# A decoder trunk's feed-forward stage: ordinary work in ready pieces, held transposes, second products added onto used banks

## The chip, the cores and the metric

The kernel runs on one core of a Trainium2 chip. The core has a matrix engine (TensorE, PE in the profile; its weight loads are PEld), a vector engine (VectorE, DVE), a scalar engine (ScalarE, ACT), a general one (GpSimd, POOL) and a queue engine (SyncE, SP) that issues most transfers here. Each engine works through its own list of instructions and waits on semaphores for the others. The metric is the device time of one execution in microseconds (us); lower is better.

## The reference

Two decoder layers over 256 tokens of width 2048, all in float32:

```python
for l in range(DEPTH):                       # 2
    h = rms_norm(x, norm1_g[l])
    z = h @ w_in[l]                          # 2048 -> 3584
    out_a = chunked_sgu(gelu(z[..., :2048]), ...)
    out_b = swa_sink_attention(z[..., 2048:3072], z[..., 3072:3328], z[..., 3328:], ...)
    mixed = concatenate([rms_norm(out_a, ...), rms_norm(out_b, ...)])
    x = x + mixed @ w_out[l]                 # 2048 -> 2048
    h2 = rms_norm(x, norm2_g[l])
    x = x + (silu(h2 @ w_gate[l]) * (h2 @ w_up[l])) @ w_down[l]   # 2048 -> 5632 -> 2048
```

Only the last two lines, the feed-forward stage, are touched by the change.

## The kernel before

**Precision.** Every float32 product is made from three products of a shorter format (fp32r). `split2` (L93) turns a loaded weight tile `raw` of 128 x 1024 into a high part `wh` (a copy on ScalarE, L99) and a low part `wl` (a subtraction on VectorE, L100). `mm3` (L137) issues high x high, high x low and low x high (L138 to L140), each 512 columns wide, into one bank of PSUM, the memory that TensorE adds its results up in. Activations are stored split in the same way, transposed, in tiles called `hT` and `aT`.

**Two kinds of work.** The hidden width of 5632 is 11 blocks of 512 columns.

- Eight blocks (`S_BLOCKS`, 3 to 10) use `seven` (L587), a Strassen-like scheme: two token halves times gate and up weights, in seven products where eight are usual. Its first phase takes five products into five banks `m0` to `m4` over four steps `i`, with sums of weight tiles made on VectorE (L613, L614, L619) and one more sum made by an adding transfer from GpSimd's queue (L621). Then the banks are combined on VectorE (L629 to L638) and two more products are taken in a second phase, L642 to L648, into two new banks `n0` and `n1`. Each block has 28 units (`s_unit`, one split and 6 matmuls each): 20 in the first phase, 8 in the second. At the end come a Silu on ScalarE (L652), products with the up part on VectorE (L654), and transposes through `act_T` (L573).
- The other three blocks, 0 to 2, use `gate_up` (L674) in the ordinary way: 8 units (one split and 12 matmuls each) of gate weights, then 8 of up weights. The down projection of all 11 blocks, `down` (L689), is ordinary too: for each of four column blocks `n` it adds up the blocks that it is given and adds the result to the residual `xres` (L704). Both use the accumulators `dacc`, two banks; a following piece starts when VectorE or ScalarE has read the ones before.

An s_unit needs much of VectorE (its split and the sums) and little of TensorE; an ordinary unit needs one split for twice the matmuls. So the two are mixed.

**The order.** The instructions are written out by two generators. `s_stream` (L661) goes through the eight blocks, one s_unit at a time. `std_stream` (L711) goes through `STD_ORDER` (L44): block 0's gate and up, down of blocks 0 and 3, and so on, in that order only. A planner keeps a `debt`: `vec` (L109) adds the cost of vector work (1.14 for a split or a sum, 0.6 for a smaller one), `pe` (L112) takes off 0.227 x LOAD for each matmul. After each s_unit, ordinary units are written for as long as the debt is above zero (L720). If the next ordinary piece lacks an input, `std_stream` yields False and only s_units are written, one after another, until the input is there.

**Transposes.** `act_later` (L583) puts a block's two transposes off by 2 and 3 ticks of a clock that an ordinary unit moves by 1 and an s_unit by 0.5. `act_T` then writes four transposes of 128 x 128 on TensorE into the single bank `sm`, a copy on ScalarE (L577) and a subtraction on VectorE (L578) into an `aT` tile. There are six `aT` tiles (ACTS), and each block of 512 needs two until its down projection is done.

**Buffers** that matter: seven `raw` tiles, five each of `wh` and `wl`, five banks in the pool `pa` (tag `acc`: `m0` to `m4`, `n0`, `n1`), two in `pd` (`dacc`), one in `pm` (`sm`), eight vector-sized tiles `z`. The compiler gives a tile its slot when one is free, and may set an instruction that is ready ahead of an earlier one that is not.

Of the kernel before, what the change touches and what calls it, by code (L numbers as in the profile page):

```python
# [12 lines left out]
F32 = mybir.dt.float32  # L13
# [8 lines left out]
P = 128  # L22
# [3 lines left out]
L = 2  # L26
# [15 lines left out]
ND = D // NB  # L42
S_BLOCKS = (3, 4, 5, 6, 7, 8, 9, 10)
STD_ORDER = (  # L44
    ("gu", 0), ("down", (0, 3)), ("gu", 1), ("down", (1, 4)), ("down", (5, 6)), ("gu", 2),
    ("down", (2, 7)), ("down", (8, 9)), ("down", (10,)),
)
ACTS = 6
VEC = 1.14
VEC_P = 0.6  # L50
MM = 0.227
LOAD = 0.91
RL = 512
WARM = 12

# [12 lines left out]
def trunk(ctx, tc, x, xt, w_in, w_out, w_gate, w_up, w_down, sgu_w, sgu_g, consts,  # L68
# [39 lines left out]

    def vec(n, cost=VEC):  # L109
        debt[0] += n * cost  # L110
# [7 lines left out]
    def later(delay, fn):  # L118
        pending.append((clock[0] + delay, next(serial), fn))
# [8 lines left out]
    def new_acc(pool=pa, tag="acc"):  # L128
        return [pool.tile([P, NB], F32, tag=tag, name=f"{tag}{t}") for t in range(NTOK)]
# [7 lines left out]
    def mm3(acc, ah, al, wh, wl, first, last):  # L137
        nc.tensor.matmul(acc, ah, wh, start=first, stop=False)  # L138
        nc.tensor.matmul(acc, ah, wl, start=False, stop=False)  # L139
        nc.tensor.matmul(acc, al, wh, start=False, stop=last)  # L140

    def unit(src, acts, acc, first, last):
        raw = raw_load(src, 2 if clock[0] < 4 else 1)
# [131 lines left out]
    for lay in range(L):  # L275
# [297 lines left out]
        def act_T(b, c, sg, pairs_f=pairs_f):  # L573
            ps = pm.tile([P, 2, SEQ], F32, tag="sm", name="ps_f")
            transpose_pair([sg[t][:, 2 * c * P : (2 * c + 2) * P] for t in range(NTOK)], ps)
            pair = pair_tile("aT")
            nc.scalar.copy(pair[:, 0], ps)  # L577
            nc.vector.tensor_tensor(pair[:, 1], ps, f(pair[:, 0]), ALU.subtract)  # L578
            vec(1, VEC_P)
            pe(2)  # L580
            pairs_f.setdefault(b, []).append(pair)

        def act_later(b, sg, act_T=act_T):  # L583
            for c in range(2):
                later(2 + c, lambda c=c: act_T(b, c, sg))

        def seven(b, lay=lay, pairs2=pairs2, ext2=ext2, act_later=act_later):  # L587
            bank = [pa.tile([P, NB], F32, tag="acc", name=f"m{i}") for i in range(5)]

            def s_unit(raw, m, i, op, first, last):  # L590
                wh, wl = split2(raw)
                for j in range(2):
                    ah, al = (op(2 * i + j, h) for h in range(2))
                    mm3(bank[m], ah, al, wh[:, j, :], wl[:, j, :], first and j == 0, last and j == 1)
# [35 lines left out]
            nc.scalar.copy(m1, bank[0])  # L630
            u1 = zp.tile([P, NB], F32, tag="z", name="u1")
            nc.vector.tensor_tensor(u1, bank[3], m1, ALU.add)
            c22 = zp.tile([P, NB], F32, tag="z", name="c22")
            c21 = zp.tile([P, NB], F32, tag="z", name="c21")
            nc.vector.tensor_tensor(c21, bank[2], u1, ALU.add)
            nc.vector.tensor_tensor(c22, bank[1], c21, ALU.add)
            nc.vector.tensor_tensor(u1, bank[1], u1, ALU.add)
            nc.vector.tensor_tensor(u1, bank[4], u1, ALU.add)  # L638
            vec(5, VEC_P)
            yield  # L640
            bank = [pa.tile([P, NB], F32, tag="acc", name=f"n{i}") for i in range(2)]
            for i in range(4):  # L642
                b21 = raw_load(w_gate[lay, b, i, 1])
                first, last = i == 0, i == 3
                s_unit(b21, 0, i, a_op(1, 0), first, last)
                yield
                s_unit(kept[i], 1, i, a_op(1, 1), first, last)
                yield  # L648
            sg = [m1, c21]
            for t, m in ((0, m1), (1, c21)):  # L650
                nc.vector.tensor_tensor(m, bank[t], m, ALU.add)
                nc.scalar.activation(m, m, AF.Silu, scale=rstd2[t])  # L652
            for t, c in ((0, u1), (1, c22)):
                nc.vector.scalar_tensor_tensor(sg[t], c, nrstd2[t], sg[t], ALU.mult, ALU.mult)  # L654
            vec(4, VEC_P)
            act_later(b, sg)
            yield

# [12 lines left out]
                    yield True  # L671
            return acc

        def gate_up(b, even=even, act_later=act_later):  # L674
            acc = yield from even(b, w_gate)
            sg = []
            for t in range(NTOK):
                s = zp.tile([P, NB], F32, tag="z", name="sg")
                nc.scalar.activation(s, acc[t], AF.Silu, scale=rstd2[t])  # L679
                sg.append(s)  # L680
            acc = yield from even(b, w_up)
            for t in range(NTOK):
                nc.vector.scalar_tensor_tensor(
                    sg[t], acc[t], rstd2[t], sg[t], ALU.mult, ALU.mult
                )
            vec(NTOK, VEC_P)
            act_later(b, sg)

        def down(blocks, final, lay=lay, pairs_f=pairs_f, norm_block=norm_block, ss1=ss1, pairs1=pairs1):  # L689
            for n in range(ND):  # L690
                while any(len(pairs_f.get(b, [])) < 2 for b in blocks):
                    yield False
                acc = new_acc() if seven_done[0] else new_acc(pd, "dacc")
                for k, b in enumerate(blocks):
                    for c in range(2):
                        pair = pairs_f[b][c]
                        unit(
                            w_down[lay, b, n, c], [(pair, 0), (pair, 1)], acc,
                            k == 0 and c == 0, k == len(blocks) - 1 and c == 1,
                        )  # L700
                        yield True
                for t in range(NTOK):
                    xs = xres[:, t, n * NB : (n + 1) * NB]
                    nc.vector.tensor_tensor(xs, acc[t], xs, ALU.add)  # L704
                    vec(1, VEC_P)
                    if final and lay == L - 1:
                        nc.sync.dma_start(out[t * P : (t + 1) * P, n * NB : (n + 1) * NB], xs)
                if final and lay < L - 1:
                    norm_block(n, ss1, pairs1, lay + 1, C_G1)

        def std_stream(gate_up=gate_up, down=down):  # L711
            for k, (kind, what) in enumerate(STD_ORDER):
                if kind == "gu":
                    yield from gate_up(what)
                else:
                    yield from down(what, k == len(STD_ORDER) - 1)
# [98 lines left out]
```

## Time and profile before

| | us |
|---|---|
| median of 3 runs | 1961.52 |
| lowest, highest | 1959.99, 1965.34 |
| the profiled execution | 1963.79 |
| its span | 1962.1 |

The first matmuls of the seven-product blocks stand at 288 us in the first layer and at 1264 us in the second; before them lie the input projection, the two mixers and the output projection of each layer.

A row of the profile names the line, the engine, the operation and the tiles as output<-inputs. In the timeline the columns are start, duration, engine, line, operation and tiles, shape, count, and in brackets the idle time before the instruction with what ended it. In the table by windows each engine stands with its busy time and, in brackets, the number of its instructions that touch the window, in the order PE, PEld, DVE, ACT, POOL; behind them the granted clock of TensorE, the share of the DMA engines and GB/s. A group's row has busy time and mean duration in ns, then the idle time before its instructions and what ended it. A row of the list of waits has the waiting engine and line, what it waited for, the sum in us, the count and the longest.

### The profile page before, as it was taken

Reading aid. Unit: us, or ns where it says so; the run is one execution under the profiler, and the core shown is the slowest. Engines: PE = TensorE matmul, PEld = TensorE weight load, DVE = VectorE, ACT = ScalarE, POOL = GpSimd, SP = SyncE. Lnnn points to the kernel's source line nnn. Section 1 sums busy time; section 2 is a strip of 40 time slices with the busy share of each in tenths; the row PEclk is TensorE's granted clock in tenths of the full one; section 3 lists DMA queues with packets and bytes.
Section 4 is the critical chain, followed back from the end, with each engine's and each line's share of the span. In section 5 each row is a group of like instructions: output and inputs, shape, how many; then the busy total and the mean of one; then the engine's idle time right before and its main releaser. Section 6 shows DMA issues by size and latency. Waiting matters only on the chain.

```text
span 1962.1 us, 24613 instructions
## 1 busy us (share of the span) xinstructions
PE 1947.1 (99%) x8942; PEld 1596.4 (81%) x8942; DVE 1660.7 (85%) x1883; ACT 1131.1 (58%) x1429; POOL 120.3 (6%) x129
## 2 busy tenths in 40 slices
PE   9999999999999999999999999999999999999999
PEld 7788888878878888888888888888888788888887
DVE  6776689989989899999667866899899898999984
ACT  7465566655655556656455565666556565565562
POOL 1210000000000000000002100000000000000000
PEclk9999999999999999999999999999999999999999
DMA  8854558677686776867655455676776767767773
GB/s 319 270 167 154 189 165 245 202 235 215 219 257 207 230 239 198 255 220 244 195 187 192 158 162 183 185 232 195 234 234 222 242 213 226 238 216 253 217 244 108
DMA packets 118554, 420.22 MB, mean 214 GB/s; under 512 B 13040, under 2 KB 15216, under 8 KB 118432
## 3 DMA queue, kind: packets, MB, share of 16 engines
q1 hardware_dynamic: 106928, 377.57, 55.7%
q0 software_dynamic: 11360, 41.00, 11.8%
q8 instruction: 70, 1.15, 0.2%
q14 instruction: 52, 0.43, 0.1%
q10 hardware_dynamic: 144, 0.08, 0.0%
HBM read 416.47 MB, written 4.23 MB: 214 GB/s over the span
## 4 chain that ended last, share of the span: by engine, by line
PE 88%; DVE 7%; DMA 3%; issue 2%; ACT 1%; POOL 0%; SPq 0%; ACTq 0%; DVEq 0%
PE dacc L138 10%; PE dacc L139 10%; PE dacc L140 10%; PE acc L138 9%; PE acc L140 9%; PE acc L139 9%; PE m L140 6%; PE m L139 6%; PE m L138 6%; DVE wl L100 3%; PE n L140 3%; PE n L139 3%; PE n L138 3%; PE ps_v L399 1%; DMA raw<-in_w_in_dram 1%
## 5 line engine op out<-in xcount | busy, mean ns | idle before, releaser
L99 ACT CAST wh<-raw 128x1024 fp32r<-128x1024 f32 (+1 forms) x770 | 794.1, 1049 | 657.4 <-PE acc L140 162.9
L100 DVE TENSOR_TENSOR wl<-raw,wh 128x1024 fp32r<-128x1024 f32 (+1 forms) x770 | 920.2, 1218 | 193.3 <-ACT wh L99 184.7
L138 PE MATMUL dacc<-wh,aT 128*128 128x512 f32 x576 | 225.2, 393 | 4.1 <-DVE xres L704 3.6
L139 PE MATMUL dacc<-wl,aT 128*128 128x512 f32 x576 | 225.0, 391 | 0.0
L140 PE MATMUL dacc<-wh,aT 128*128 128x512 f32 x576 | 224.8, 390 | 0.0
L139 PE MATMUL m<-wl,ext 128*128 128x512 f32 x512 | 200.6, 392 | 1.2 <-DVE wl L100 1.1
L138 PE MATMUL m<-wh,ext 128*128 128x512 f32 x512 | 200.1, 391 | 0.4 <-ACT wh L99 0.4
L140 PE MATMUL m<-wh,ext 128*128 128x512 f32 x512 | 199.4, 389 | 0.0
L138 PE MATMUL acc<-wh,hT 128*128 128x512 f32 x448 | 180.3, 404 | 0.2 <-ACT wh L99 0.2
L139 PE MATMUL acc<-wl,hT 128*128 128x512 f32 x448 | 175.4, 391 | 0.8 <-DVE wl L100 0.8
L140 PE MATMUL acc<-wh,hT 128*128 128x512 f32 x448 | 175.3, 391 | 0.0
L99 ACT CAST wh<-t 128x1024 fp32r<-128x1024 f32 x128 | 134.7, 1053 | 49.3 <-PE dacc L140 26.3
L100 DVE TENSOR_TENSOR wl<-t,wh 128x1024 fp32r<-128x1024 f32 x128 | 155.8, 1217 | 8.2 <-ACT wh L99 5.3
L138 PE MATMUL dacc<-wh,hT 128*128 128x512 f32 x384 | 151.1, 394 | 1.4 <-ACT sg L679 1.1
L138 PE MATMUL acc<-wh,aT 128*128 128x512 f32 x384 | 151.3, 394 | 0.0
L140 PE MATMUL acc<-wh,aT 128*128 128x512 f32 x384 | 149.8, 390 | 0.0
L139 PE MATMUL dacc<-wl,hT 128*128 128x512 f32 x384 | 149.7, 390 | 0.0
L140 PE MATMUL dacc<-wh,hT 128*128 128x512 f32 x384 | 149.7, 390 | 0.0
L139 PE MATMUL acc<-wl,aT 128*128 128x512 f32 x384 | 149.7, 390 | 0.0
L621 POOL DMA_DIRECT2D t<-in_w_gate_dram x64 | 54.7, 854 | 1337.8 <-DVE wl L100 769.7
L138 PEld LDWEIGHTS dacc<-wh,aT 128*128 128x128 f32 x576 | 107.7, 188 | 29.5 <-DVE xres L704 6.2
L139 PEld LDWEIGHTS dacc<-wl,aT 128*128 128x128 f32 x576 | 108.2, 188 | 22.9 <-DVE wl L100 0.8
(150 smaller groups left out, 2973.4 us busy)
## 6 DMA issues: line engine op xcount, KB each, us to landing
raw<-in_w_gate_dram SPq DMA_DIRECT2D x176, 512.0 KB, 5.5
raw<-in_w_up_dram SPq DMA_DIRECT2D x176, 512.0 KB, 4.5
raw<-in_w_down_dram SPq DMA_DIRECT2D x176, 512.0 KB, 4.6
raw<-in_w_in_dram SPq DMA_DIRECT2D x108, 512.0 KB, 4.5
raw<-in_w_out_dram SPq DMA_DIRECT2D x64, 512.0 KB, 3.3
t<-in_w_gate_dram POOLq DMA_DIRECT2D x64, 512.0 KB, 7.2
bias<-rdram POOLq DMA_DIRECT2D x8, 512.0 KB, 5.4
raw<-in_w_in_dram SPq DMA_DIRECT2D x8, 256.0 KB, 5.6
```

Of the source, the lines that this page charges most:

```text
L99: nc.scalar.copy(wh[:, j : j + step, :], src)
L100: nc.vector.tensor_tensor(wl[:, j : j + step, :], src, f(wh[:, j : j + step, :]), ALU.subtract)
L138: nc.tensor.matmul(acc, ah, wh, start=first, stop=False)
L139: nc.tensor.matmul(acc, ah, wl, start=False, stop=False)
L140: nc.tensor.matmul(acc, al, wh, start=False, stop=last)
L399: nc.tensor.matmul(pv[:, i, :], pt[:, i * nkb + b, :], zkv[b][:, (NKV + g) * HD : (NKV + g + 1) * HD], start=b == 0, stop=b == nkb - 1,)
L621: nc.gpsimd.dma_start(t2, w_gate[lay, b, i, 1], accum_op=ALU.add)
```

## The change

Three things change in the feed-forward stage, and two constants.

1. Ordinary work is cut into pieces: a gate half or an up half of a block, or one column block `n` of a down projection. `std_stream` keeps a list of them in the old order and each time takes the first one whose inputs are there. Only one block may be between its gate and its up half.
2. `act_later` no longer writes a transpose at its due time as such. It is put in `held` and written (`admit`) as soon as `room` says that one of the six `aT` tiles will be free for it, with tiles set aside for earlier down projections. When a down projection has ended, its tiles count as freed and `admit` is called. At the end of a first phase (`yield last`) ordinary work is also written while more than HOLD = 2 transposes are held.
3. In `seven` the second phase adds its two products onto banks 0 and 2 of the first phase (`start` is False throughout), after those banks have been read. The combination of the banks is reordered to suit, and needs two VectorE additions less for each block. The products of `kept` tiles come one step later. Banks are taken when they are first written.
4. LOAD goes from 0.91 to 0.90; HOLD is new.

```diff
-LOAD = 0.91
+HOLD = 2
+LOAD = 0.90
...
+        held = []
+        made = []
+        freed = [0]
+        chunks = [what for kind, what in STD_ORDER if kind == "down"]
+
+        def room(b, made=made, freed=freed):
+            at = next(i for i, c in enumerate(chunks) if b in c)
+            missing = sum(2 - made.count(x) for c in chunks[:at] for x in c)
+            return len(made) - freed[0] + missing < ACTS
+
+        def admit(act_T=act_T, held=held, made=made, room=room):
+            for e in list(held):
+                if room(e[0]):
+                    held.remove(e)
+                    made.append(e[0])
+                    act_T(*e)
+
+        def act_later(b, sg, held=held, admit=admit):
+            def come(c):
+                held.append((b, c, sg))
+                admit()
+
             for c in range(2):
-                later(2 + c, lambda c=c: act_T(b, c, sg))
+                later(2 + c, lambda c=c: come(c))
...
-            bank = [pa.tile([P, NB], F32, tag="acc", name=f"m{i}") for i in range(5)]
+            bank = {}
...
                 s_unit(b22, 4, i, e_op(3), first, last)
-                yield
                 kept.append(t2)
+                yield last
             m1 = zp.tile([P, NB], F32, tag="z", name="m1")
             nc.scalar.copy(m1, bank[0])
             u1 = zp.tile([P, NB], F32, tag="z", name="u1")
             nc.vector.tensor_tensor(u1, bank[3], m1, ALU.add)
+            c12 = zp.tile([P, NB], F32, tag="z", name="c12")
             c22 = zp.tile([P, NB], F32, tag="z", name="c22")
-            c21 = zp.tile([P, NB], F32, tag="z", name="c21")
-            nc.vector.tensor_tensor(c21, bank[2], u1, ALU.add)
-            nc.vector.tensor_tensor(c22, bank[1], c21, ALU.add)
-            nc.vector.tensor_tensor(u1, bank[1], u1, ALU.add)
-            nc.vector.tensor_tensor(u1, bank[4], u1, ALU.add)
-            vec(5, VEC_P)
+            nc.vector.tensor_tensor(c12, bank[1], u1, ALU.add)
+            nc.vector.tensor_tensor(c22, bank[2], c12, ALU.add)
+            nc.vector.tensor_tensor(c12, bank[4], c12, ALU.add)
+            vec(4, VEC_P)
             yield
-            bank = [pa.tile([P, NB], F32, tag="acc", name=f"n{i}") for i in range(2)]
-            for i in range(4):
-                b21 = raw_load(w_gate[lay, b, i, 1])
-                first, last = i == 0, i == 3
-                s_unit(b21, 0, i, a_op(1, 0), first, last)
-                yield
-                s_unit(kept[i], 1, i, a_op(1, 1), first, last)
-                yield
-            sg = [m1, c21]
-            for t, m in ((0, m1), (1, c21)):
-                nc.vector.tensor_tensor(m, bank[t], m, ALU.add)
-                nc.scalar.activation(m, m, AF.Silu, scale=rstd2[t])
-            for t, c in ((0, u1), (1, c22)):
+            for i in range(5):
+                if i < 4:
+                    b21 = raw_load(w_gate[lay, b, i, 1])
+                    s_unit(b21, 0, i, a_op(1, 0), False, i == 3, skip_group_check=True)
+                    yield
+                if i > 0:
+                    s_unit(kept[i - 1], 2, i - 1, a_op(1, 1), False, i == 4, skip_group_check=True)
+                    yield
+            sg = [m1, u1]
+            nc.vector.tensor_tensor(u1, bank[2], u1, ALU.add)
+            for t, src in ((0, bank[0]), (1, u1)):
+                nc.scalar.activation(sg[t], src, AF.Silu, scale=rstd2[t])
+            vec(1, VEC_P)
+            for t, c in ((0, c12), (1, c22)):
                 nc.vector.scalar_tensor_tensor(sg[t], c, nrstd2[t], sg[t], ALU.mult, ALU.mult)
-            vec(4, VEC_P)
+            vec(2, VEC_P)
             act_later(b, sg)
...
+            if n == ND - 1:
+                freed[0] += 2 * len(blocks)
+                admit()
+
+        def std_stream(half=half, down=down, pairs_f=pairs_f):
+            pieces = []
+            for kind, what in STD_ORDER:
+                if kind == "gu":
+                    sg = []
+                    pieces += [((), half, (what, True, sg)), ((), half, (what, False, sg))]
+                else:
+                    last = what == chunks[-1]
+                    pieces += [(what, down, (what, n, last)) for n in range(ND)]
+            begun = set()
+            while pieces:
+                for k, (need, fn, args) in enumerate(pieces):
+                    if any(len(pairs_f.get(b, [])) < 2 for b in need):
+                        continue
+                    if fn is half and not args[1] and args[0] not in begun:
+                        continue
+                    if fn is half and args[1] and begun:
+                        continue
+                    break
+                else:
                     yield False
+                    continue
+                pieces.pop(k)
+                if fn is half:
+                    (begun.add if args[1] else begun.discard)(args[0])
+                yield from fn(*args)
...
-        for _ in s_stream():
-            while debt[0] > 0.0 and next(other, False):
+        for full in s_stream():
+            while (debt[0] > 0.0 or full and len(held) > HOLD) and next(other, False):
                 pass
```

`half` is one half of the old `gate_up`, and `down` now does one column block `n` for each call; the instructions in them are the old ones.

More of the change, by code (lines that the diff above doesn't have):

```diff
@@ L135, in small_ps, with mm3 @@
         return pool.tile(shape, F32, tag=tag, name=name)
[L137 to L140, printed above, removed]
+    def mm3(acc, ah, al, wh, wl, first, last, **more):
+        nc.tensor.matmul(acc, ah, wh, start=first, stop=False, **more)
+        nc.tensor.matmul(acc, ah, wl, start=False, stop=False, **more)
+        nc.tensor.matmul(acc, al, wh, start=False, stop=last, **more)
     def unit(src, acts, acc, first, last):
@@ L672, in even, with half @@
             return acc
-        def gate_up(b, even=even, act_later=act_later):
-            acc = yield from even(b, w_gate)
-            sg = []
+        def half(b, gate, sg, even=even, act_later=act_later):
+            acc = yield from even(b, w_gate if gate else w_up)
             for t in range(NTOK):
[L678 to L681, printed above, removed]
-            for t in range(NTOK):
[L683 to L687, printed above, removed]
@@ L689, in down @@
-        def down(blocks, final, lay=lay, pairs_f=pairs_f, norm_block=norm_block, ss1=ss1, pairs1=pairs1):
-            for n in range(ND):
-                while any(len(pairs_f.get(b, [])) < 2 for b in blocks):
-                    yield False
[L693 to L716, printed above, removed]
+                if gate:
+                    s = zp.tile([P, NB], F32, tag="z", name="sg")
+                    nc.scalar.activation(s, acc[t], AF.Silu, scale=rstd2[t])
+                    sg.append(s)
+                else:
+                    nc.vector.scalar_tensor_tensor(
+                        sg[t], acc[t], rstd2[t], sg[t], ALU.mult, ALU.mult
+                    )
@@ new lines, in half, with down @@
+            if not gate:
+                vec(NTOK, VEC_P)
+                act_later(b, sg)
+        def down(blocks, n, final, lay=lay, pairs_f=pairs_f, norm_block=norm_block, ss1=ss1,
+                 pairs1=pairs1, freed=freed, admit=admit):
+            acc = new_acc() if seven_done[0] else new_acc(pd, "dacc")
+            for k, b in enumerate(blocks):
+                for c in range(2):
+                    pair = pairs_f[b][c]
+                    unit(
+                        w_down[lay, b, n, c], [(pair, 0), (pair, 1)], acc,
+                        k == 0 and c == 0, k == len(blocks) - 1 and c == 1,
+                    )
+                    yield True
+            for t in range(NTOK):
+                xs = xres[:, t, n * NB : (n + 1) * NB]
+                nc.vector.tensor_tensor(xs, acc[t], xs, ALU.add)
+                vec(1, VEC_P)
+                if final and lay == L - 1:
+                    nc.sync.dma_start(out[t * P : (t + 1) * P, n * NB : (n + 1) * NB], xs)
+            if final and lay < L - 1:
+                norm_block(n, ss1, pairs1, lay + 1, C_G1)
+            if n == ND - 1:
+                freed[0] += 2 * len(blocks)
+                admit()
```

11 lines of the change are left out of this document (6 added, 5 removed).

## The prediction

> **What bounds the kernel now.** I read the page's busy shares first, then the waits of TensorE, then TensorE's own rows, and last the windows that show where it lags.
>
> ```profile
> PE 1947.1 (99%) x8942; PEld 1596.4 (81%) x8942; DVE 1660.7 (85%) x1883; ACT 1131.1 (58%) x1429; POOL 120.3 (6%) x129
> PEclk9999999999999999999999999999999999999999
> PE dacc L138 <- DVE xres L704: 3.8, 4, 1.5
> ```
>
> TensorE is the bound, at full granted clock in every slice, and its longest wait in the list sums to 3.8 us. But a matmul's row is longer than its share of the engine, so the pace has to be read from starts.
>
> ```profile
> 401.24 0.39 PE L140 MATMUL dacc<-wh,aT 128*128 128x512 f32 x1
> ...
> 402.60 0.39 PE L140 MATMUL dacc<-wh,aT 128*128 128x512 f32 x1
> 402.82 0.39 PE L138 MATMUL m<-wh,ext 128*128 128x512 f32 x1
> 403.76 0.50 PE L139 MATMUL m<-wl,ext 128*128 128x512 f32 x1 [0.55 <-DVE wl L100]
> 405.50 0.50 PE L138 MATMUL dacc<-wh,aT 128*128 128x512 f32 x1 [1.24 <-DVE xres L704]
> 454.08 0.44 PE ps_f L208 x4
> ```
>
> From 401.24 to 402.60 lie six starts: 0.2267 us a matmul of 512 columns. Then the steps are 0.94 and 1.74 us, so 0.71 and 1.51 us are lost, though the idle shown in brackets is less. Four transposes take 0.44 us, 0.11 each. With these two prices a window's lost time can be counted: its length plus the 0.39 us of the one row that hangs over its edge, less 0.2267 for each matmul and 0.11 for each transpose. Below, five windows of all instructions (the second number behind PE is the count), then the transposes inside three of them; in the other places the program writes eight too, two pairs of four.
>
> ```profile
> 378.00:412.00 34.00, 31.73 (x141) 25.11 (x140) 29.77 (x29) 16.40 (x18) 1.69 (x2) 1.00 0.74 228
> 555.00:590.00 35.00, 33.49 (x150) 26.98 (x149) 28.27 (x30) 18.89 (x21) 1.71 (x2) 1.00 0.78 247
> 816.00:850.00 34.00, 34.00 (x157) 28.14 (x156) 31.70 (x35) 20.21 (x23) 0.06 (x1) 1.00 0.68 219
> 1355.00:1390.00 35.00, 33.67 (x150) 26.91 (x149) 31.60 (x31) 18.39 (x20) 1.70 (x2) 1.00 0.75 236
> 1531.00:1560.00 29.00, 28.41 (x127) 22.51 (x126) 25.28 (x25) 15.88 (x18) 1.70 (x2) 1.00 0.85 261
> 412.00:555.00 143.00, 143.00 (x637) 117.56 (x636) 131.50 (x128) 85.82 (x90) 5.96 (x7) 1.00 0.72 226
> 378.00:412.00 34.00, 1.20 (x8) 0.99 (x8) 1.36 (x2) 1.16 (x2) 1.00 0.74 228
> 816.00:850.00 34.00, 1.47 (x11) 1.40 (x12) 1.37 (x2) 1.16 (x2) 1.00 0.68 219
> 412.00:555.00 143.00, 2.72 (x16) 2.12 (x16) 2.74 (x4) 2.34 (x4) 1.00 0.72 226
> ```
>
> Lost: 34.39 - 133 x 0.2267 - 0.88 = 3.4 us; then 2.3, 2.3 and 1.5 us in the windows from 555, 1355 and 1531; together 9.5 us in 133 us. The stretch from 412 to 555 loses 143.39 - 621 x 0.2267 - 1.76 = 0.85 us, 0.6%; the window from 816 loses 0.1 us. So TensorE stands close to its floor except at four short places, two in each layer.
>
> **What happens there.** I stepped the debt rule through the blocks by the constants of the code. A layer's seven-product stream has 8 blocks of 28 units. The other stream is refused (its generator yields False) over units 35 to 41, 96 to 102 and 186 to 192: at `("down", (0, 3))` it waits for block 0's transposes, which fall due 2 and 3 ticks after its gate/up units; at `("down", (1, 4))` for block 1's; at `("down", (2, 7))` for block 2's. Meanwhile the debt climbs from 1.45 to 4.46, and six ordinary units are then written in one run. The rows of VectorE show it.
>
> ```profile
> 382.62 0.74 DVE sg L683
> 389.23 0.68 DVE L578 TENSOR_TENSOR aT<-ps_f,aT 128x512 fp32r<-128x512 f32 x1
> 392.70 4.62 DVE L100 TENSOR_TENSOR wl<-raw,wh 128x1024 fp32r<-128x1024 f32 x4
> 401.35 3.50 DVE L100 TENSOR_TENSOR wl<-raw,wh 128x1024 fp32r<-128x1024 f32 x3 [4.03 <-ACT wh L99]
> 404.76 1.28 DVE L704 TENSOR_TENSOR xres<-dacc,xres 128x512 f32<-128x512 f32 x2
> 400.27 3.89 ACT L99 CAST wh<-raw 128x1024 fp32r<-128x1024 f32 x4 [6.38 <-PE dacc L140]
> ```
>
> Block 0's gate/up ends at 382.62, its first transposed tile comes at 389.23; in between only seven-product units run. In the run of ordinary units ScalarE fills the weight buffers, then stands 6.38 us until TensorE frees one; the splits for the next units and the two `xres` adds that free the accumulators come too late behind it (three splits at 401.35 ahead of the adds at 404.76), and TensorE waits at 402.82 and 403.76.
>
> **The change part by part.**
>
> *Order of ordinary work.* The piece list goes on to the next piece whose inputs are there. With the new constants block 0's second half ends at unit 36; `down (0, 3)` is not ready, so the gate half of block 1 starts, and block 0's transposes fall under it. After block 1's second half (unit 97) the gate half of block 2 does the same. After block 2's second half (unit 188) nothing is left that could run: refused until 194, as now. There the debt stays at 2.0 to 2.4 instead of 4.9 and the window of that place loses 0.1 us now, so I price it at nothing. The two other places go in each layer: 9.5 less the 0.6% of 133 us that any stretch loses, -8.7 us. The matmuls, loads and transposes stay the same in number.
>
> *Held transposes.* Six `aT` tiles exist. When block 6 is done (unit 112) the tiles of 4, 5 and 1 fill them, so 6 and then 7 are held until the fourth piece of `down (1, 4)` ends (unit 147), and four transposes come in a row through the one bank of `sm`. Never more than two entries are held where the stream says `full`, so HOLD decides nothing.
>
> ```profile
> L577 ACT CAST aT<-ps_f 128x512 fp32r<-128x512 f32 x44 | 25.6, 582 | 20.2 <-PE ps_f L208 14.5 <-PE dacc L140 5.6
> L578 DVE TENSOR_TENSOR aT<-ps_f,aT 128x512 fp32r<-128x512 f32 x44 | 30.1, 683 | 3.0 <-ACT aT L577 2.8
> L630 ACT COPY m<-m 128x512 f32<-128x512 f32 x16 | 9.3, 583 | 3.5 <-PE m L140 3.5
> L651 DVE TENSOR_TENSOR m<-n,m 128x512 f32<-128x512 f32 x16 | 10.9, 682 | 0.0
> L652 ACT ACTIVATE m<-m,ir 128x512 f32<-128x512 f32 x16 | 11.6, 724 | 12.5 <-DVE m L651 12.5
> L99 ACT CAST wh<-t 128x1024 fp32r<-128x1024 f32 x128 | 134.7, 1053 | 49.3 <-PE dacc L140 26.3 <-PE n L140 7.6 <-PE m L140 4.6
> ```
>
> A transpose must wait until the one ahead has left the bank: 0.58 + 0.68 us behind its 0.44, so three waits of 1.26 us at most, 3.8 us a layer if TensorE has nothing else in its queue. Three ordinary units of 12 matmuls (8.2 us) are written right behind, whose inputs (block 5's tiles) are old; whatever of them goes between the transposes hides the waits. Queued behind them are the splits on ScalarE and VectorE. The wait that ends, 5.6 us of ScalarE behind `dacc` for a tile, cost TensorE nothing that the rows show. Bounds 0 to 7.6 us for both layers; I take 2, near the covered end, since the units that cover are in the same queue.
>
> *Second products onto used banks.* Nothing is added to TensorE. VectorE loses two adds a block: of nine instructions behind the products seven are left, 32 x 0.682 = 21.8 us in all. TensorE's 99% hides them, so I count 0; with VectorE as the bound they would be worth 21.8 us. The next thing to ask is whether bank 0 and bank 2 are late. Bank 0 is read by the copy (L630), bank 2 by one add; both come before the splits of the unit that adds to them on the same in-order engines, so no wait is new. Today the second pair takes freed banks of the same pool of five, under the same condition. At a block's end:
>
> ```profile
> 521.96 0.68 DVE L651 TENSOR_TENSOR m<-n,m 128x512 f32<-128x512 f32 x1
> 522.12 0.39 PE L140 MATMUL n<-wh,hT 128*128 128x512 f32 x1
> 522.56 0.68 DVE L651 TENSOR_TENSOR c<-n,c 128x512 f32<-128x512 f32 x1
> 523.73 0.70 ACT L652 ACTIVATE c<-c,ir 128x512 f32<-128x512 f32 x1
> 524.35 1.98 ACT L99 CAST wh<-raw 128x1024 fp32r<-128x1024 f32 x2
> 525.07 0.39 PE L138 MATMUL m<-wh,hT 128*128 128x512 f32 x1
> ```
>
> The last product starts at 522.12, and the next block's goes on at 525.07, with one ordinary unit of 12 matmuls (2.72 us) between: no gap. The chain that this unit covers is add 0.68, Silu 0.72, split 1.05 = 2.45 us. By the debt rule one ordinary unit follows most block ends in the changed kernel (two or more in half of them today), and none follows block 5's. Bounds there: 0 to 2.45 us for each layer; I take 0.5, because splits prepared ahead cover 5 buffers.
>
> By the Trainium skill (Perfetto Trace Analysis, section Optimizing Tensor Performance, Matmuls) independent matmul groups should rotate through banks so that one's evacuation overlaps the next one's matmuls. The change rotates less, and by that rule all 16 block ends would show the 2.45 us, 39 us in all; the rows at 522.12 speak against it, since a unit of the other stream does the overlapping whatever the bank.
>
> *The constants.* LOAD 0.90 credits a matmul less. A block now leaves a debt of 15.9 instead of 16.7, mostly through the vector work that went; 115 instead of 119 of a layer's 136 ordinary units are written before the seven-product stream ends, 21 instead of 17 after it. A stretch of ordinary units alone has room:
>
> ```profile
> 1900.00:1950.00 50.00, 50.00 (x226) 41.29 (x225) 31.92 (x35) 20.66 (x22) 0.00 (x0) 1.00 0.48 158
> ```
>
> TensorE is never short there, VectorE is 64% busy: 0 for the four units.
>
> **The sum** is made on the profiled execution: its 1963.8 us (span 1962.1 and 1.7 around it) - 8.7 + 2 + 1 = 1958.1. That execution lies 2.3 above the median 1961.5, and its two layers differ by 1.9 us at the same places, so such stalls vary by that much; I carry over the difference, -5.7, and round: 1955.5 us.
>
> **Rivals.** *The stalls move.* The row of four transposes at its upper price (7.6) and both block ends (4.9) give -8.7 + 12.5 = +3.8; half of that price gives -2.5: 1959 to 1965, 1959 likeliest. For it: VectorE is 88 to 92% busy in the windows above (29.77 of 34 us, 131.50 of 143), so an order that bunches its work shows on TensorE. Against it: debt stays under 2.6 throughout, and runs of six units end.
>
> *The block ends are laid bare* (slower). ScalarE is in order; the Silu of bank 2 waits for the add, and that for the last product; if the next block's split stands behind it and the ordinary unit's too, TensorE loses 2.45 us. It eats the gain from 4 exposed ends of 16, and makes the kernel slower by over 0.3% from 6; with half of them, -5.7 + 8 x 2.45 = +13.9: 1975. For it: fewer ordinary units follow each end. Against it: no wait of this kind is in the list now.
>
> *The change does nothing:* the pieces come in the old order because the transposes happen to be due in time, and the refusals stay: 1961.5. My count says otherwise, but it is a count of the written order; the engines' order is set again by the compiler.
>
> **How the numbers follow.** Forecast 0.57, stalls that move 0.20, block ends 0.13, nothing 0.10. A change under 0.3% (5.9 us) can't be told from none here. The forecast lies at -6 with some 3 us to either side; half of it would count as faster, and I put three quarters there, because VectorE's relief of 21.8 us, counted at 0, can only add to the gain, together with a little of the second case: 0.45. Same: the rest of the forecast, most of the second case and all of the last, 0.38. Slower 0.17: the block ends and a part of the second. Range: 1951 (all 9.5 us and a little of the other loss gone, nothing new) to 1964 (the second case with most of its price); the forecast's own range is 1952 to 1959.
>
> **What would show it.** Right: in windows of 30 us around the ends of the two gate/up blocks 0 and 1, the loss is under 0.5 us; between the two halves' rows of block 1 no stretch without `dacc` matmuls longer than ten seven-product units; VectorE's busy time falls by about 22 us and its count by 32. Wrong: waits of `ps_f` transposes of over 1 us around the end of `down (1, 4)`; a wait of an `m` matmul for a split right behind the Silu; a granted clock under 1.0. A time under 1951 would mean that VectorE bound the stretches which I called full.

## The result, and the profile after

| | us |
|---|---|
| before, median of 5 runs | 1959.99 (1959.78 to 1965.34) |
| after, median of 5 runs | 1953.78 (1953.10 to 1955.40) |
| ratio, after to before | 0.9962, 95% interval 0.9948 to 0.9977 |
| profiled execution after, its span | 1953.11, 1951.4 |

The three runs of the table ahead of the prediction are among the five of the kernel before. The kernel is faster by 0.38%: 6.2 us by the medians, 7.4 by the means (1961.3 and 1953.9), which the ratio follows. The two profiled executions lie 10.7 us apart (1963.79 and 1953.11).

The page of the kernel after has these shares of busy time:

```profile
PE 1943.2 (100%) x8942; PEld 1596.7 (82%) x8942; DVE 1643.8 (84%) x1851; ACT 1134.9 (58%) x1429; POOL 120.3 (6%) x129
...
PEclk9999999999999999999999999999999999999999
```

TensorE has the same 8942 matmuls, VectorE 32 instructions less and 17 us less busy time. The chain that ended last (the work followed back from the end, each step to what it had waited for) tells more. First its shares in the kernel before, then in the kernel after:

```profile
PE 88%; DVE 7%; DMA 3%; issue 2%; ACT 1%; POOL 0%; SPq 0%; ACTq 0%; DVEq 0%
```

```profile
PE 99%; DMA 0%; DVE 0%; ACT 0%; issue 0%; SPq 0%; DVEq 0%; ACTq 0%
```

Before, the end could be followed back through VectorE and through transfers; now it is TensorE for 99% of the span. The next two views serve to count the lost time of the four places by the prediction's formula. First the windows of the kernel before, each one about a seven-product block (the second and the fourth of each layer), and the transposes in them:

```profile
363.00:447.00 84.00, 81.73 (x365) 66.53 (x364) 74.28 (x73) 45.58 (x49) 3.38 (x4) 1.00 0.71 219
525.00:611.00 86.00, 84.49 (x379) 69.01 (x378) 78.27 (x78) 49.37 (x53) 3.41 (x4) 1.00 0.71 220
1340.00:1423.00 83.00, 81.67 (x366) 66.68 (x365) 74.47 (x73) 45.85 (x49) 3.39 (x4) 1.00 0.71 222
1501.00:1586.00 85.00, 84.41 (x377) 68.71 (x376) 78.27 (x77) 49.41 (x53) 3.41 (x4) 1.00 0.71 223
363.00:447.00 84.00, 2.39 (x16) 1.88 (x16) 2.72 (x4) 2.33 (x4) 1.00 0.71 219
525.00:611.00 86.00, 2.59 (x17) 2.22 (x18) 2.74 (x4) 2.33 (x4) 1.00 0.71 220
```

Then the same blocks after, and the transposes of the first:

```profile
360.00:439.00 79.00, 78.91 (x356) 64.72 (x355) 71.56 (x68) 48.80 (x53) 3.38 (x4) 1.00 0.70 227
516.00:597.00 81.00, 81.00 (x365) 66.66 (x364) 73.98 (x71) 48.70 (x52) 3.41 (x4) 1.00 0.71 227
1330.00:1409.00 79.00, 78.90 (x356) 64.77 (x355) 71.60 (x69) 48.86 (x52) 3.38 (x4) 1.00 0.70 226
1486.00:1567.00 81.00, 81.00 (x366) 66.63 (x365) 74.01 (x71) 48.73 (x52) 3.40 (x4) 1.00 0.72 227
360.00:439.00 79.00, 2.40 (x16) 1.99 (x16) 2.74 (x4) 2.32 (x4) 1.00 0.70 227
```

For the first row before: 84.39 - 349 x 0.2267 - 16 x 0.11 = 3.5 us; then 2.5, 2.3 and 1.8 us, 10.0 us together (the two layers' blocks hold 16 transposes, one window 17). After: 79.39 - 340 x 0.2267 - 1.76 = 0.6, then 0.5, 0.6 and 0.3 us, 1.9 us together. The four places gave 8.1 us. The spans lie 10.7 us apart (1962.1 and 1951.4), so no other place took it back, and about 2.6 us went elsewhere. The longest wait of an `m` or `dacc` matmul that is left in the list after is this one:

```profile
PE m L139 <- DVE wl L100: 0.4, 1, 0.4
```

### The profile page after: what moved, and what is told of

It reads as the page before. It is cut to its first block, busy times and chain, and to the rows that moved or that the text cites. A ratio compares the mean times of both kernels' runs of the same rounds, so it can differ in the third digit from the quotient of the medians.

```text
span 1951.4 us, 24555 instructions
## 1 busy us (share of the span) xinstructions
PE 1943.2 (100%) x8942; PEld 1596.7 (82%) x8942; DVE 1643.8 (84%) x1851; ACT 1134.9 (58%) x1429; POOL 120.3 (6%) x129
## 4 chain that ended last, share of the span: by engine, by line
PE 99%; DMA 0%; DVE 0%; ACT 0%; issue 0%; SPq 0%; DVEq 0%; ACTq 0%
PE dacc L138 11%; PE dacc L139 11%; PE dacc L140 11%; PE m L139 10%; PE m L140 10%; PE m L138 10%; PE acc L138 10%; PE acc L140 10%; PE acc L139 10%; PE ps_v L399 1%; PE ps_f L208 1%; PE ps_s L357 1%; PE ps_t L208 1%; PE ps_p L392 1%; PE ps_n L208 1%; PE ps_g L441 0%
## 5 line engine op out<-in xcount | busy, mean ns | idle before, releaser
L138 PE MATMUL dacc<-wh,aT 128*128 128x512 f32 x544 | 212.5, 392 | 0.0
L139 PE MATMUL dacc<-wl,aT 128*128 128x512 f32 x544 | 212.5, 391 | 0.0
L140 PE MATMUL dacc<-wh,aT 128*128 128x512 f32 x544 | 212.4, 390 | 0.0
L138 PE MATMUL acc<-wh,aT 128*128 128x512 f32 x416 | 164.2, 395 | 0.0
L140 PE MATMUL acc<-wh,aT 128*128 128x512 f32 x416 | 162.3, 390 | 0.0
L139 PE MATMUL acc<-wl,aT 128*128 128x512 f32 x416 | 162.1, 390 | 0.0
L138 PE MATMUL m<-wh,hT 128*128 128x512 f32 x384 | 150.0, 390 | 0.0
L140 PE MATMUL m<-wh,hT 128*128 128x512 f32 x384 | 149.6, 390 | 0.0
L139 PE MATMUL m<-wl,hT 128*128 128x512 f32 x384 | 149.4, 389 | 0.0
```

Source lines behind the costliest of these rows:

```text
L138: nc.tensor.matmul(acc, ah, wh, start=first, stop=False, **more)
L139: nc.tensor.matmul(acc, ah, wl, start=False, stop=False, **more)
L140: nc.tensor.matmul(acc, al, wh, start=False, stop=last, **more)
```

## The experiments

The first question was which part pays: the order of ready pieces, the held transposes, the used banks with VectorE's relief, or the constants.

**The piece list alone.** The kernel before with the new `std_stream`, `half` and `down`, without `held`. The first lines show the new generator against the old one; the last three stand in the changed kernel and are left out here:

```diff
-        def std_stream(gate_up=gate_up, down=down):
+        def std_stream(half=half, down=down, pairs_f=pairs_f):
+            pieces = []
...
-            if n == ND - 1:
-                freed[0] += 2 * len(blocks)
-                admit()
```

> The kernel before with the piece list alone: first ready piece next, transposes written at their due time, second products into new banks, LOAD 0.91. By the debt rule the ordinary stream is refused only over units 186 to 191 of a layer, and no run of six ordinary units is left. Theory (the loss sits in the refusals and the runs of ordinary units after them): ratio to before 0.996 to 0.997, the windows at the ends of gate/up blocks 0 and 1 lose under 0.7 us each. Rival A (the gain is VectorE's relief by 32 additions): ratio 1.000. Rival B (the gain is that no transpose waits for a tile): ratio 1.000.

Measured: 1953.90 us against 1962.90 beside it, ratio 0.9951 (0.9938 to 0.9963), a little better than expected. This part alone is enough for all of the gain.

**Used banks, old order.** The kernel before with the new second phase, but with the old costs written into the debt. Against `seven` of the changed kernel these two lines differ:

```diff
-            vec(4, VEC_P)
+            vec(5, VEC_P)
...
-            vec(1, VEC_P)
+            vec(2, VEC_P)
```

> The kernel before with the second products added onto banks 0 and 2 and two VectorE additions fewer a block, but with the old costs in the debt (5 and 4 small ones), so that the units are written in the old order, refused at units 35, 96 and 186. Theory: ratio 0.999 to 1.000, and the two places a layer still lose 1.5 to 3.5 us each. Rival A: ratio 0.996 to 0.997. Rival C (the banks lay the block ends bare): ratio over 1.002 in this kernel, where nothing else pays for it.

Measured: 0.9983 (0.9974 to 0.9992), 1960.14 us. This lies between the theory and rival A: a small gain, so the banks cost nothing here and the block ends are not bare.

**Holding alone**, with old pieces and old banks:

```diff
-                later(2 + c, lambda c=c: act_T(b, c, sg))
+                later(2 + c, lambda c=c: come(c))
```

> The kernel before with transposes held until one of six tiles is free, old order of pieces, old banks, LOAD 0.91. The ordinary stream is refused as before (35, 96, 186). Theory: ratio 0.999 to 1.001. Rival B: ratio 0.996 to 0.997.

Measured: 0.9992 (0.9983 to 1.0001). No effect that can be told from none, as the theory said.

**The changed kernel with the old order of pieces:**

```diff
-        def std_stream(half=half, down=down, pairs_f=pairs_f):
+        def std_stream(gate_up=gate_up, down=down):
+            for k, (kind, what) in enumerate(STD_ORDER):
...
```

> The changed kernel with its ordinary pieces in the old fixed order; holding, banks and LOAD 0.90 as changed. Refused over units 36 to 41, 97 to 102 and 188 to 193; runs of six and of four ordinary units after the first two. Theory: most of the loss comes back, ratio 0.998 to 1.000, the first place loses 2 to 3.5 us in each layer and the second less. Rival A: ratio 0.996 to 0.997.

Measured: 0.9954 (0.9941 to 0.9966), 1954.39 us. This is a clear miss. The ordinary stream is refused at the same three places as before, the run of six is still written after the first, and the time is that of the changed kernel. The same four blocks lose 1.2, 0.5, 1.2 and 0.5 us here, 3.4 us together. The first of them, with 16 transposes (81.39 - 346 x 0.2267 - 1.76 = 1.2):

```profile
360.00:441.00 81.00, 80.76 (x362) 66.08 (x361) 72.76 (x70) 46.04 (x49) 3.39 (x4) 1.00 0.71 227
```

So the refusal is not in itself what costs most.

**Relief and delay.** Four more kernels were built: the changed kernel without the used banks (old `seven`, and without the clause on HOLD); the changed kernel with the additions of `c12` and `c22` done twice; and both kernels with transposes due three ticks later.

```diff
-            nc.vector.tensor_tensor(c12, bank[1], u1, ALU.add)
-            nc.vector.tensor_tensor(c22, bank[2], c12, ALU.add)
+            for _ in range(2):
+                nc.vector.tensor_tensor(c12, bank[1], u1, ALU.add)
+            for _ in range(2):
+                nc.vector.tensor_tensor(c22, bank[2], c12, ALU.add)
```

```diff
-                later(2 + c, lambda c=c: act_T(b, c, sg))
+                later(5 + c, lambda c=c: act_T(b, c, sg))
```

> The changed kernel with the old combination and the second products into two new banks (32 more VectorE additions); piece list, holding and LOAD 0.90 as changed. Refused only over units 176 to 181, debt up to 4.55 there. Theory: ratio 0.996 to 0.9975, that place costs under 1 us as the third place did before. Rival A: ratio 0.999 to 1.000.

> The changed kernel with the additions of c12 and c22 done twice: the 32 VectorE additions of about 0.68 us are back, the debt does not know of them, so the units are written in the same order. Theory: VectorE's relief is covered by TensorE, 0 to +1 us against the changed kernel, ratio to before 0.996 to 0.997. Rival A: +5 to +7 us, ratio about 1.000.

> The kernel before with the transposes of every block due 5 and 6 ticks after it and not 2 and 3. Refused over 12 units and not 6 (35 to 46, 96 to 107, 186 to 197), debt up to 8.5, then runs of 8, 7 and 8 ordinary units. Theory: the loss grows with the refusal, each of the places loses 4 to 8 us, third ones too: +10 to +30 us, ratio 1.005 to 1.015. Rival D (the places lose by chance of the compiled order, not by the refusal): under +3 us, ratio 0.999 to 1.0015.

> The changed kernel with the transposes due 5 and 6 ticks after a block. Refused only over units 188 to 199, debt up to 6.9, then a run of 7. Theory: the piece list hides the delay at two of three places, so one place a layer loses 3 to 6 us: +5 to +12 us against the changed kernel, ratio to before 0.999 to 1.002, and at least 8 us faster than the kernel before with the same delay. Rival D: as the changed kernel, 0.996 to 0.997.

| kernel | median, us | ratio to before, 95% |
|---|---|---|
| changed, without the used banks | 1951.82 | 0.9946 (0.9932 to 0.9960) |
| changed, additions doubled | 1954.16 | 0.9959 (0.9946 to 0.9972) |
| before, transposes later | 1984.78 | 1.0110 (1.0096 to 1.0125) |
| changed, transposes later | 1960.07 | 0.9985 (0.9976 to 0.9994) |

Rival A falls twice: 32 more additions leave the time where it was, and without the banks it is not slower but faster, by more than was expected. Rival D falls too: making the refusal 12 units long and not 6 or 7 costs 22 us in the old order, and about 4.5 us in the new one (0.9985 against 0.9962). In the new order only one refusal in a layer is left to grow, so the piece list does hide such a delay; the ratio 0.9985 lies just under the 0.999 expected.

**What parts the fast kernels from the slow ones.** ScalarE's waits for the transfers of `w_down`. In the list of waits of the kernel before, then of the used banks in the old order, then of holding alone (the columns are the sum in us, the number, the longest):

```profile
ACT wh L99 <- DMA raw<-in_w_down_dram: 13.3, 4, 5.2
```

```profile
ACT wh L99 <- DMA raw<-in_w_down_dram: 15.6, 5, 4.5
```

```profile
ACT wh L99 <- DMA raw<-in_w_down_dram: 18.5, 7, 4.7
```

In the piece list alone, the changed kernel in the old order and the one without the used banks these waits sum to only 0.7, 1.4 and 0.6 us; in the changed kernel to this:

```profile
ACT wh L99 <- DMA raw<-in_w_down_dram: 1.5, 4, 0.7
```

The sum does not rank the kernels by itself: it is 5.6 us with the additions doubled (ratio 0.9959), and 10.6 us, less than in the kernel before, with the transposes late in the old order (1.0110).

In the kernel before, the waits lie in the runs of ordinary units behind the refusals. Rows of ScalarE in the kernel before:

```profile
575.54 2.95 ACT L99 CAST wh<-raw 128x1024 fp32r<-128x1024 f32 x3 [4.72 <-DMA raw<-in_w_down_dram]
1376.09 2.95 ACT L99 CAST wh<-raw 128x1024 fp32r<-128x1024 f32 x3 [5.17 <-DMA raw<-in_w_down_dram]
```

And the chain of waits of the kernel before, in the window that ends with the stall at 581:

```profile
568.71 6.74 DMA raw<-in_w_down_dram
...
575.54 1.06 ACT wh L99
576.60 0.02 issue
576.62 2.36 DVE wl L100 x2
578.98 0.52 DVE u L632
579.50 1.12 DVE wl L100
580.63 0.01 issue
580.63 0.69 DVE xres L704
581.33 0.04 issue
581.37 0.50 PE dacc L138
```

A weight tile lands at 575.4 after 6.74 us (4.6 is the median of these loads on the page); ScalarE stood for it, VectorE splits it late, the `xres` adds that free the accumulators queue behind those splits, and TensorE's next `dacc` matmul waits.

The first place of the first layer, where the prediction saw ScalarE wait 6.38 us for TensorE until 400.27, fits this too. The tile that ScalarE takes up there was asked for at 392.20 and landed 8.0 us later, at 400.2 (the first row is SyncE's issue, the second its size and its time to landing):

```profile
392.20 0.33 SPq L90 DMA_DIRECT2D raw<-in_w_down_dram  x1
...
raw<-in_w_down_dram SPq DMA_DIRECT2D x1, 512.0 KB, 8.0
```

Two kernels were built from the one before to tell the transfers from the hand-over of the accumulators, both with the refusals kept:

```diff
                 if final and lay < L - 1:
                     norm_block(n, ss1, pairs1, lay + 1, C_G1)
+                if not seven_done[0]:
+                    yield False
```

> The kernel before, but a run of ordinary units ends when an accumulator is handed over (the generator yields False after each half and each column block), so that one seven-product unit stands between a column block's last matmul and the next one's first; refusals at units 35, 96 and 186 stay. The fast and slow kernels so far part by one row, ScalarE's waits for transfers of w_down (13 to 19 us in the three slow ones, 0 to 1.5 in the fast ones). Theory F (the transfers of the run come late, and the accumulators are only what waits last): most of the loss stays, 1.5 us or more in each of the four places together with at least 8 us of ScalarE waiting for w_down, ratio to before 0.998 to 1.000. Theory G (the hand-over inside the run is the loss): under 0.8 us a place, ratio 0.995 to 0.9965.

```diff
             for n in range(ND):
+                here = None
+                if blocks in ((0, 3), (1, 4)) and n < 2:
+                    here = f(pairs2[0]).rearrange("p h j s -> p h (j s)")
```

> The kernel before, where the first two column blocks of the down projections (0, 3) and (1, 4) in each layer take their weights from a tile that lies in SBUF already (a transposed activation tile), so that the run after each refusal needs no transfers: 32 loads of w_down fewer, and those products are computed on other data. Refusals, runs, hand-overs, splits and matmuls stay. Theory F: under 0.8 us a place, no wait of ScalarE for w_down over 2 us in all, ratio 0.995 to 0.997. Theory G, or VectorE's load in the refused stretch: 1.5 to 3 us a place, ratio 0.9985 to 1.000.

In the second one the run takes its weights from a tile that lies in SBUF, so these products are computed on other data. Both measured 0.9975, with 0.9966 to 0.9984 and 0.9965 to 0.9984: 4.9 us of 1962.2. That is between what theory F and theory G allowed, in both kernels. With the weights in SBUF the waits for `w_down` sum to 0.5 us, and the same four blocks are these, with their transposes:

```profile
363.00:444.00 81.00, 80.52 (x360) 65.84 (x359) 73.63 (x72) 45.50 (x49) 3.39 (x4) 1.00 0.60 176
522.00:607.00 85.00, 84.98 (x383) 69.52 (x382) 79.03 (x79) 49.93 (x54) 3.40 (x4) 1.00 0.58 173
1335.00:1416.00 81.00, 80.52 (x359) 65.86 (x358) 73.67 (x72) 45.53 (x49) 3.39 (x4) 1.00 0.59 175
1494.00:1578.00 84.00, 83.95 (x376) 68.71 (x376) 78.08 (x78) 49.46 (x53) 3.41 (x4) 1.00 0.59 176
363.00:444.00 81.00, 1.94 (x14) 1.49 (x12) 2.74 (x4) 2.32 (x4) 1.00 0.60 176
522.00:607.00 85.00, 2.90 (x20) 2.53 (x20) 2.74 (x4) 2.33 (x4) 1.00 0.58 173
1335.00:1416.00 81.00, 1.79 (x12) 1.49 (x12) 2.74 (x4) 2.33 (x4) 1.00 0.59 175
1494.00:1578.00 84.00, 2.55 (x16) 2.04 (x16) 2.74 (x4) 2.33 (x4) 1.00 0.59 176
```

81.39 - 346 x 0.2267 - 14 x 0.11 = 1.4 us, then 0.9, 1.4 and 1.0: 4.7 us where the kernel before loses 10.0 and the changed one 1.9. So the late transfers carry some two thirds of what the change gained (5.3 of 8.1 us in the blocks, 4.9 of about 7 us in the times). That kernel also has 32 loads fewer on the queues, so that the other loads may gain from it as well. In its trace the stalls inside the runs of ordinary units (at 403.76, 405.50, 581.37, 1381.32 and 1547.71 in the kernel before, about 6 us by TensorE's starts) have no counterpart; what is left stands earlier, in the refused stretch, at the first place of each layer. TensorE's rows there in the kernel before, then in this one:

```profile
388.23 0.50 PE L138 MATMUL m<-wh,ext 128*128 128x512 f32 x1 [0.21 <-ACT wh L99]
391.10 0.50 PE L139 MATMUL m<-wl,ext 128*128 128x512 f32 x1 [0.28 <-DVE wl L100]
```

```profile
387.66 0.50 PE L138 MATMUL m<-wh,ext 128*128 128x512 f32 x1 [0.21 <-ACT wh L99]
390.54 0.50 PE L139 MATMUL m<-wl,ext 128*128 128x512 f32 x1 [0.28 <-DVE wl L100]
```

By their starts each of these waits costs about 0.55 us, in both kernels. So the refusal does cost something by itself, some 1.1 us at the first place of each layer, where the splits do not keep up; the 6 us in the runs go with the late transfers. The hand-overs stayed in that kernel and cost nothing, which speaks against theory G. It does not bear out theory F in full either, since under 0.8 us a place was expected. The broken run can't decide between the two, because a run that stops at the hand-over also asks for four tiles and not six; it too has none of these stalls in the four blocks. It still waits 3.1 us once for `w_down`, and TensorE stalls for a split elsewhere:

```profile
PE m L139 <- DVE wl L100: 2.8, 4, 1.1
```

**The changed kernel beside the one without the used banks**, on one chip:

> The changed kernel itself, beside the next one on one chip. All theories: ratio to before 0.995 to 0.9965.

> The changed kernel without the used banks (as in the run of that name before), on the same chip as the changed kernel. If the used banks cost time that the piece list pays for: 1.5 to 2.5 us under the changed kernel. If they are free: within 1 us of it. If VectorE's relief is worth something: over it.

Measured: 1954.91 us (0.9964, 0.9951 to 0.9977) and 1951.79 us (0.9950, 0.9936 to 0.9964). The version without the used banks is faster than both kernels of this study, by 3.1 us against the changed one. In that profile the changed kernel has a new small stall, shown in TensorE's rows and ScalarE's:

```profile
1442.76 0.39 PE L138 MATMUL m<-wh,ext 128*128 128x512 f32 x1
1444.02 0.50 PE L139 MATMUL m<-wl,ext 128*128 128x512 f32 x1 [0.87 <-DVE wl L100]
```

```profile
1439.38 1.05 ACT L99 CAST wh<-raw 128x1024 fp32r<-128x1024 f32 x1 [1.71 <-DMA raw<-in_w_down_dram]
```

The step of 1.26 us holds 1.03 us of loss, behind a late `w_down` tile once more, in a run of three ordinary units. In this profile the changed kernel's waits for `w_down` sum to 3.7 us, those of the version without the banks to 0.9. Whether the banks do this or the debt that they leave (115 ordinary units before the end of the seven-product stream against 124) was not tried.

## Why the prediction was right, and where not

*The size.* Forecast -5.7 us, carried to 1955.5; measured 1953.8, a difference of 6.2 us by the medians and 7.4 by the ratio. (1961.5 - 5.7 is 1955.8; the 1955.5 of the prediction is rounded too far.) The term of -8.7 us for four places measured -8.1 us in the blocks that hold them, and windows of 30 us right behind the ends of gate/up blocks 0 and 1 (382:412, 555:585, 1352:1382, 1525:1555) lose 0.0 to 0.3 us, under the 0.5 that the prediction named. But this term was read off the windows as lost time, whatever its cause, so its coming true does not show that the cause was right; that it came out so well although the cause was partly another is luck.

*The added costs* were set too high. The row of four transposes, 2 us: no matmul waits for it in the list after, and holding alone measured 0.9992. The block ends, 1 us: no wait of this kind, and the used banks alone measured 0.9983. VectorE's busy time fell by 17 us and not by 22. Counting its relief at nothing held: with the additions put back the ratio is 0.9959 against 0.9962 and 0.9964. The 39 us that would have come from bare block ends at all 16 places have nothing in these runs for them. That HOLD decides nothing was not run by itself; stepping the planner without the clause writes the same order.

*The step that failed* is the one between the refusal and the stall. The prediction read ScalarE's 6.38 us, shown as a wait for `dacc`, as full weight buffers: "In the run of ordinary units ScalarE fills the weight buffers, then stands 6.38 us until TensorE frees one". At the sister places the same wait is shown as one for a transfer of `w_down`, the tile of this place landed 8.0 us after its issue, just before ScalarE went on, and taking the transfers away took about half of the blocks' loss (10.0 to 4.7 us) and all of the stalls in the runs. Full buffers could not have held ScalarE so long either: TensorE works off an ordinary unit in 12 x 0.2267 = 2.7 us. The prediction also held the refusal for the cause. The changed kernel in the old order keeps every refusal and a run of six, and its four blocks lose 3.4 us, not 10.0. Removing refusals is one way to keep the loads in time (the piece list alone: 0.9951); a changed mix with the old order is another (0.9954). What brings the loads of that run in early enough, one seven-product unit further on, was not settled. Of the rest, a part comes from the refused stretch itself (the rows at 388.23 and 391.10), and it grows with the refusal: with the transposes late in the old order TensorE's largest wait is for ScalarE's half of a split.

```profile
PE m L138 <- ACT wh L99: 7.8, 10, 2.1
```

*Slips in the working.* VectorE is 81 to 93% busy in the windows that the prediction lists, not 88 to 92%. The count of bare block ends that would eat the gain (4, and 6 for a slower kernel) goes by -8.7 us, the time of 1975 by -5.7; by -5.7 it would be 3 and 5. Neither enters the forecast.

*The rivals.* The stalls did move a little (1 us at 1442.8 in one profile), far less than the 1959 of that case. The block ends stayed covered, and the order did change. What the second rival needs is seen once: with the transposes late in the old order a block ends inside the long refusal, where no ordinary unit follows, and TensorE stands 2.10 us (at 839.41, in the last section).

## What to carry to other kernels

Where one engine is at its floor, count the starts at its steady pace and look for the windows that fall short; the gain to be had is their sum, and it sits in a few places. A wait shown for an engine that had just finished may be a late transfer: look at the sister places of the same code, and at when the transfer landed, before naming the cause. In a planner that mixes two streams, keep runs of the transfer-hungry kind short, and let it take the next ready piece when the first one is late.

## What the hardware showed that was not expected

With the transposes late in the old order, TensorE's clock halved three times in the middle of the work. Two windows of that kernel around the first time (TensorE's granted clock is the third number from the end):

```profile
838.00:840.00 2.00, 0.50 (x1) 0.19 (x1) 2.00 (x4) 1.69 (x2) 0.00 (x0) 0.98 0.00 0
840.00:842.00 2.00, 1.64 (x4) 1.20 (x5) 2.00 (x4) 2.00 (x3) 0.00 (x0) 0.50 0.00 0
```

And TensorE's rows there, the last one from the second time:

```profile
836.91 0.40 PE L140 MATMUL m<-wh,hT 128*128 128x512 f32 x1
839.41 0.50 PE L138 MATMUL m<-wh,ext 128*128 128x512 f32 x1 [2.10 <-ACT wh L99]
840.36 1.22 PE L138 MATMUL dacc<-wh,aT 128*128 128x512 f32 x2 [0.45 <-ACT wh L99]
841.38 0.63 PE L139 MATMUL m<-wl,ext 128*128 128x512 f32 x1
841.80 0.63 PE L140 MATMUL m<-wh,ext 128*128 128x512 f32 x1
...
1399.43 0.51 PE L138 MATMUL dacc<-wh,aT 128*128 128x512 f32 x1 [1.98 <-DVE xres L704]
```

No wait was longer than 2.10 us, yet the clock stood at 0.50 between 840 and 842 and the matmuls started 0.42 us apart. The Trainium skill (TensorE: Matmul & The Clock Gate, Part 1: The HAM clock gate) has the clock fall back after at least one idle window of about 3.4 us; here matmuls in between did not prevent it. The second time it followed one wait of 1.98 us, at 1399.43: the granted clock is 0.50 from 1399.73 to 1403.14. It does not always come so: in the kernel with used banks in the old order a wait of 2.03 us at 578.55 left the clock at 1.00. A stall of 2 us can thus cost more than itself. In the profiled executions before and after, the clock is full for as long as TensorE works.
